# Down-projection weights prepared beside the mixers, and FFN evacuations put ahead, in a one-core hybrid-mixer step

## The chip, the cores and the metric

One core of one Trainium2 chip. The core has a matmul engine (TensorE: PE, with its weight loads PEld), a vector engine (VectorE: DVE), an activation engine (ScalarE: ACT), a general engine (GpSimd: POOL) and SyncE (SP), which in this kernel only issues DMA transfers. The metric is the device time of one execution in microseconds (us); the median of several runs counts.

## The reference

One layer over 2048 prompt tokens behind 16 meta tokens, and over 8 sample sequences of 4 tokens with states of their own. Width 1024. Three mixers run side by side on parts of the projected width, then an output product, then a SwiGLU FFN of inner width 2816:

```python
y, st = _mixer(_rmsnorm(h, norm_mix[l]), p, init_states[l], kv)
h = h + y
h = h + _swiglu(_rmsnorm(h, norm_ffn[l]), w_ffn_in[l], w_ffn_out[l])
...
# _mixer
proj = hn @ w_in
...
oa, s_hgrn_new = _hgrn2_chunked(qa, ka, ai.reshape(B, T, H_A, DV_A), logf, s_hgrn)
...
hm, c_new, n_new, m_new = _mlstm_chunked(qm, km, vm, igate, lfgate, c0, n0, m0)
...
yc = _swa_prompt(qc, kc, vc, sk)          # the sample part: _swa_sample
y = jnp.concatenate([ya, yb, yc], axis=-1) @ w_out
...
# _swiglu
g, u = jnp.split(hn @ w_ffn_in, 2, axis=-1)
return (jax.nn.silu(g) * u) @ w_ffn_out
```

The results are the normalised outputs of prompt and sample tokens, and the mixers' final states.

## The kernel before

The tokens are cut in 17 tiles: tiles 1 to 16 of 128 prompt tokens, and tile 0 with the 32 sample and 16 meta tokens. Large products take fp16 operands, each number split in a high and a low half, in three passes (high·high, high·low, low·high). `split_w` makes the halves: ACT writes the high one, then one DVE operation writes the low one.

The order in time:

1. *Start.* `w_in` is loaded and split.
2. *Mixers.* For each tile, `project(t)` makes the projections, and `mixer_prompt` runs sliding-window attention, mLSTM and HGRN2 as generators, a step of each in turn (`interleave`). The mixed tile `yT` goes to DRAM. Tile 16 comes later.
3. *Out products.* The sample mixer, tile 16's mixer and `out_early` run together. For each pair of tiles `out_product` loads `yT` (as `xT`), multiplies by `w_out` and adds the residual. Seven of the eight pairs are also normalised here, and `prep` makes their FFN operands x2 and stores them. `load_x2` then brings those of group 1 back, by DMA transposes.
4. *FFN*, in three groups of tiles: 1 to 6, 7 to 12, and 13 to 16 with tile 0. Both FFN products are done as Strassen-like 2x2 block products: seven products instead of eight, whose operands are blocks and their sums (`S1` to `S4` of the left operand, `T1` to `T4` of the right one). The inner width has 11 steps `jq` of 256, in parts of 2, 3, 3 and 3. In a part `hidden` (matmuls `s`, evacuated to `tmp`, results hi and lo to `hh`) runs for each of its steps, and then `down` (matmuls `dn`) for both halves `m` of the output and each pair of tiles. So there are four transitions from hidden to down in each group.

In group 1 the weights' operands are made as they are needed. `gu_operands` (gate and up) loads `raw`, forms four sums on POOL (`left`) and splits them: 44 makes, of which two are done before the group. `dn_operands` (down) does the same with `right`: 22 makes. Each has three pairs of ACT and DVE operations of 512, 256 and 1024 columns, and one store of 896 KB to `wgu_scratch` or `wdn_scratch`. Groups 2 and 3 load the operands from there.

The order of the work on each engine is set by a scheduler: it goes by the order in which the program issues the instructions, as far as operands and buffers are there by its own model of time, and what stands inside `tc.high_priority()` goes first. Pools with a fixed number of buffers per tag (`w`: 6, `raw`: 6, `sums`: 2 in group 1) say when a buffer comes free. SP's queue holds nearly all loads and stores in one order.

Lines to follow below: L155 and L156 (`split_w`), L205 (split of an input tile), L1015 to L1018 (`left`) and L1022 to L1025 (`right`) on POOL, L1239 (`s` matmuls), L1244 to L1252 (their evacuation, of which L1248 and L1249 are POOL additions), L1262 (gate times up), L1268 and L1269 (`hh`), L1274 to L1280 (the sums S1 to S4 on POOL), L1292 (`dn` matmuls). In the mixers: L527, L549, L551 and L553 (HGRN2), L835 and L837 (attention's probabilities).

Of the kernel before, what the change touches and what calls it, by code (L numbers as in the profile page):

```python
# [17 lines left out]
P = 128  # L18
# [39 lines left out]

@with_exitstack
def trunk(ctx, tc, I, O, groups):  # L60
    nc = tc.nc
    V, S, G, T = nc.vector, nc.scalar, nc.gpsimd, nc.tensor
    n_names = [0]
# [26 lines left out]
    wdn_d = nc.dram_tensor("wdn_scratch", (NFF // 2, 2, P, 2 * 7 * 256), F16, kind="Internal").ap()  # L90
# [127 lines left out]

    def project(t, s_out):
# [37 lines left out]
        def tl(s, tag, shape, dt=F32, bufs=1):  # L257
            if s.name == "s":
                return at_("s_" + tag, shape, dt)
            return at_(tag, shape, dt, bufs)  # L260
# [117 lines left out]
        with tc.high_priority():  # L378
            for s in segs:
                sl = slice(s.fo, s.fo + s.L)  # L380
                w = NS if s.name == "s" else P
                if s.name == "s":
                    s.vb = at_("s_vb", [NS, 4, 65])
# [6 lines left out]
                V.scalar_tensor_tensor(s.gb, s.gb, 1.0, gB[: s.L], op0=ALU.add, op1=ALU.mult)  # L390
        yield
# [465 lines left out]
    def mixer_prompt(s, yT, off):  # L857
        y = zt("y", [P, 512])
        interleave(swa_prompt(s, yT, off), mlstm_prompt(s, y[:, 256:512]), hgrn_prompt(s, y[:, 0:256]))
        finish_y(y, yT, off, s.L)  # L860

# [228 lines left out]

    smp = sample_mixer(tc, nc, I, O, locals())
# [36 lines left out]
    def kept(dram, make):  # L1128
# [3 lines left out]
        if w_bufs[0] == 6:  # L1132
# [44 lines left out]
    w_gu, w_dn = I["w_ffn_in"][0], I["w_ffn_out"][0]  # L1177

# [30 lines left out]
    with (  # L1209
# [20 lines left out]
        def quad(A, n):  # L1230
# [17 lines left out]
            G.tensor_tensor(r12, r12, r22, op=ALU.add)  # L1248
            G.tensor_tensor(r22, r22, r21, op=ALU.add)  # L1249
            V.tensor_tensor(r11, prod(A12, B21), r11, op=ALU.add)  # L1250
            V.tensor_tensor(r21, prod(A22, T4), r21, op=ALU.add)
            V.tensor_tensor(r12, prod(S4, B22), r12, op=ALU.add)  # L1252
            return r11, r12, r21, r22

        def hidden(q, jq, n):

            sg = quad(gu_first.pop(0) if gu_first else gu_operands(2 * jq * P), n)
            for d in sg:
                S.activation(d, d, AF.Silu, scale=UF)  # L1259
            up = quad(gu_first.pop(0) if gu_first else gu_operands(DFF + 2 * jq * P), n)  # L1260
            for d, v in zip(sg, up):
                V.scalar_tensor_tensor(d, v, UF * HS, d, op0=ALU.mult, op1=ALU.mult)  # L1262
# [3 lines left out]
            def put(op, v):  # L1266
                hi, lo = (hh[a][:, q, op, :n] for a in range(2))
                S.activation(hi, v, AF.Copy)  # L1268
                V.tensor_tensor(lo, v, hi, op=ALU.subtract)  # L1269
# [4 lines left out]
            G.tensor_tensor(s1, a21, a22, op=ALU.add)  # L1274
            put(S1, s1)
            G.tensor_tensor(s2, s1, a11, op=ALU.subtract)
            put(S2, s2)
            G.tensor_tensor(s3, a11, a21, op=ALU.subtract)
            put(S3, s3)
            G.tensor_tensor(s4, a12, s2, op=ALU.subtract)  # L1280
# [426 lines left out]
```

## Time and profile before

| what | value |
|---|---|
| median of 3 runs | 2420.63 us (2420.12 to 2420.94) |
| the profiled execution | 2414.44 us, of which span 2412.7 us |
| mean granted TensorE clock | 0.97 |
| start, projections and mixers of tiles 0 and 1 | the first 100 us |
| mixers of most tiles, 100 to 750 us | 650 us, some 14 tiles |
| last mixers and out products, 750 to 1055 us | 305 us, DMA share 0.68 |
| FFN group 1, 1055 to 1601 us | 546 us |
| FFN group 2, 1601 to 2056 us | 455 us |
| FFN group 3, 2056 us to the end | 357 us |

The profile comes from one execution, 6 us shorter than the median of the runs. The limits of the stages are read from the first matmul of each. Busy time is given per engine and stage; where two stages do the same work, their difference shows what one of them has to wait for. The clock is the share of full speed that TensorE was granted.

### The profile page before, as it was taken

The page shows a single profiled execution, that of the slowest core. Times are in us where ns is not written, and L with a number is a line of the kernel's source. Part 1 is how long each engine was busy: PE and PEld are TensorE (multiplying, and loading weights), DVE is VectorE, ACT ScalarE, POOL GpSimd, SP SyncE. Part 2 cuts the span into 40 slices and gives each one's busy share as a digit, 9 for nine tenths or more (in the row PEclk, how much of TensorE's full clock was granted, in tenths as well). Part 3 has the DMA queues.
Part 4 walks back from the last instruction along what each step waited for, and adds up shares of the span by engine and source line. Part 5 has one row for each costly group of instructions (what it writes and reads, how often), then busy time and mean ns, then how long its engine had stood idle before and what let it go on. Part 6 is the DMA issues. An engine that isn't in the chain of part 4 may idle for free. (4 is left out here: it accounts for less than half of the span.)

```text
span 2412.7 us, 51978 instructions
## 1 busy us (share of the span) xinstructions
PE 2220.3 (92%) x20298; PEld 1607.4 (67%) x20298; DVE 1679.2 (70%) x4030; ACT 943.5 (39%) x2526; POOL 1211.7 (50%) x1629
## 2 busy tenths in 40 slices
PE   6989999999999899896989979889999999999996
PEld 6677767767776445444657556567686767888886
DVE  8788988988988756558879677746454535655546
ACT  7554455554554432334343434422212123332323
POOL 7344344444443464549778788744232324544435
PEclk9999999999999899997999989899999999999998
DMA  7232333333223755996436545684324247744441
GB/s 258 50 63 69 66 67 68 75 61 74 66 64 73 173 183 192 275 330 222 153 139 231 196 158 191 191 287 185 148 108 168 108 152 199 269 176 175 177 174 38
DMA packets 294329, 364.95 MB, mean 151 GB/s; under 512 B 203808, under 2 KB 234480, under 8 KB 294067
## 3 DMA queue, kind: packets, MB, share of 16 engines
q1 hardware_dynamic: 285090, 331.02, 43.6%
q0 software_dynamic: 4384, 15.93, 1.7%
q10 hardware_dynamic: 4608, 14.68, 1.7%
q8 instruction: 159, 2.61, 0.4%
q14 instruction: 88, 0.71, 0.1%
HBM read 212.24 MB, written 103.50 MB: 131 GB/s over the span
## 5 line engine op out<-in xcount | busy, mean ns | idle before, releaser
L1239 PE MATMUL s<-x,w 128*128 128x384 f16 (+1 forms) x5544 | 826.4, 312 | 14.8 <-DMA w<-wgu_scratch 6.2
L1239 PEld LDWEIGHTS <-w 128*128 128x128 f16 x5544 | 542.6, 98 | 296.5 <-issue 13.8
L1292 PE MATMUL dn<-w,hh 128*128 128x256 f16 (+1 forms) x4158 | 444.4, 278 | 56.0 <-ACT hh L1268 23.6
L1292 PEld LDWEIGHTS <-hh 128*128 128x128 f16 (+1 forms) x4158 | 379.6, 99 | 119.8 <-ACT hh L1268 27.8
L212 PEld LDWEIGHTS <-xT 128*128 128x128 f16 (+1 forms) x1992 | 177.4, 99 | 191.4 <-issue 25.2
L1268 ACT ACTIVATE hh<-tmp 128x384 f16<-128x384 f32 (+1 forms) x231 | 112.4, 494 | 280.4 <-DVE tmp L1262 164.5
L1248 POOL TENSOR_TENSOR tmp<-tmp,tmp 128x384 f32<-128x384 f32 (+1 forms) x66 | 65.3, 990 | 279.0 <-ACT tmp L1247 271.8
L1269 DVE TENSOR_TENSOR hh<-tmp,hh 128x384 f16<-128x384 f32 (+1 forms) x231 | 144.5, 633 | 74.2 <-ACT hh L1268 72.5
L212 PE MATMUL wo<-wo,xT 128*128 128x512 f16 x768 | 180.8, 394 | 9.5 <-DVE xn L992 4.6
L156 DVE SCALAR_TENSOR_TENSOR w<-raw,w 128x512 f16<-128x512 f32 (+1 forms) x136 | 111.9, 855 | 7.0 <-ACT w L155 6.9
L1250 DVE TENSOR_TENSOR tmp<-s,tmp 128x384 f32<-128x384 f32 (+1 forms) x66 | 34.2, 518 | 107.3 <-PE s L1239 107.3
L212 PE MATMUL d<-xT,qf 128*128 128x128 f16 (+1 forms) x1632 | 107.7, 220 | 0.0
L156 DVE SCALAR_TENSOR_TENSOR w<-sums,w 128x1024 f16<-128x1024 f32 x68 | 96.9, 1427 | 11.4 <-ACT w L155 11.4
L1259 ACT ACTIVATE tmp<-tmp 128x384 f32<-128x384 f32 (+1 forms) x132 | 61.6, 489 | 107.9 <-DVE tmp L1250 52.6
L212 PE MATMUL d<-xT,bqk 128*128 128x128 f16 (+1 forms) x1632 | 100.6, 221 | 3.2 <-DVE e L278 3.2
L1324 DVE SCALAR_TENSOR_TENSOR xr<-dn,xr 128x256 f32<-128x256 f32 x192 | 78.7, 417 | 34.4 <-PE dn L1292 30.2
L212 PEld LDWEIGHTS <-qf 128*128 128x128 f16 x1632 | 94.4, 100 | 9.1 <-issue 4.1
L212 PEld LDWEIGHTS <-bqk 128*128 128x128 f16 x1632 | 94.0, 100 | 5.4 <-issue 4.5
L212 PE MATMUL d<-xT,cq 128*128 128x128 f16 (+1 forms) x1632 | 96.2, 217 | 0.0
L212 PE MATMUL d<-bvo,xT 128*128 128x512 f16 (+1 forms) x408 | 96.2, 380 | 0.0
L1262 DVE SCALAR_TENSOR_TENSOR tmp<-tmp,tmp 128x384 f32<-128x384 f32 (+1 forms) x132 | 71.9, 558 | 34.1 <-POOL tmp L1249 32.6
L212 PE MATMUL d<-aig,xT 128*128 128x512 f16 (+1 forms) x408 | 92.4, 379 | 3.4 <-DVE g L358 3.4
(536 smaller groups left out, 4064.6 us busy)
## 6 DMA issues: line engine op xcount, KB each, us to landing
w<-wgu_scratch SPq DMA_DIRECT2D x88, 896.0 KB
wgu_scratch<-w SPq DMA_DIRECT2D x44, 896.0 KB
w<-wdn_scratch SPq DMA_DIRECT2D x44, 896.0 KB
raw<-in_w_ffn_in_dram SPq DMA_DIRECT2D x88, 256.0 KB
wdn_scratch<-w SPq DMA_DIRECT2D x22, 896.0 KB
xs<-in_x_prompt_dram SPq DMA_DIRECT2D x26, 512.0 KB
x_scratch<-pT ACTq DMA_DIRECT2D x28, 448.0 KB
raw<-in_w_ffn_out_dram SPq DMA_DIRECT2D x22, 512.0 KB
```

What stands on the lines that cost most here:

```text
L156: V.scalar_tensor_tensor(lo, src, scale, hi, op0=ALU.mult, op1=ALU.subtract)
L212: T.matmul(out, lh(k, a), rh(k, b), start=(n == 0), stop=(n == 3 * nk - 1))
L1239: T.matmul(out, A[k // 2][p][:, a, k % 2 * P : k % 2 * P + P], x2[r][:, k // 2, op, k % 2, :n], start=i == 0, stop=i == 11)
L1248: G.tensor_tensor(r12, r12, r22, op=ALU.add)
L1250: V.tensor_tensor(r11, prod(A12, B21), r11, op=ALU.add)
L1259: S.activation(d, d, AF.Silu, scale=UF)
L1262: V.scalar_tensor_tensor(d, v, UF * HS, d, op0=ALU.mult, op1=ALU.mult)
L1268: S.activation(hi, v, AF.Copy)
L1269: V.tensor_tensor(lo, v, hi, op=ALU.subtract)
L1292: T.matmul(out, hh[p][:, q, a, off : off + L], ws[q][r][:, b], start=(q, p, r) == order[0], stop=(q, p, r) == order[-1])
L1324: V.scalar_tensor_tensor(x[:L, cc], m, UD, x[:L, cc], op0=ALU.mult, op1=ALU.add)
```

## The change

Three things.

*Down weights.* A generator `dn_prep` makes the down operands in 44 pieces of 128 columns. It joins the mixers' generators: `mixer_prompt` of tiles 1 to 15 interleaves three pieces with the three mixers. A piece has three loads (64, 64 and 128 KB) into a tile `nx`, four POOL operations, one ACT and one DVE operation on 128x896, and a store of 448 KB from a tile `nw`; both tiles have one buffer. In group 1 `dn_operands` now loads two halves, like the other groups, and `down` reads them in two runs of 128 columns.

*Room.* To make place, the sample tile's projections are packed in two buffers, stored to DRAM at the end of `project(0)` (`put_away`) and loaded before the sample mixer (`take_back`), into the places of `nx` and `nw`. In the FFN the pool has seven `w` and four `raw` tiles instead of six and six. `load_x2` of group 1 is interleaved with the out products and no longer follows them.

*Priority.* `Ahead` wraps an engine so that each instruction issued through it is inside `tc.high_priority()`; the evacuations, activations and additions of `quad`, `hidden` and `down` go through it, in all three groups. In a profile of the changed kernel these instructions carry the line of the wrapper, L68.

```diff
+class Ahead:
+    def __getattr__(self, name):
+        def op(*a, **k):
+            with self.tc.high_priority():
+                return getattr(self.engine, name)(*a, **k)
+        return op
...
+    VA, SA, GA = (Ahead(tc, e) for e in (V, S, G))
...
+    def put_away():
+        for which, n, c0, c1 in SPK_PARTS:
+            nc.sync.dma_start(smp_d[which, :n, c0:c1], packed[which][:n, c0:c1])
...
+    def dn_prep(n):
+        for jq, m, u in dn_pieces[:n]:
+            x = at_("nx", [P, 8, P])
+            w = at_("nw", [P, 2, 7, P], F16)
+            b12, b11, b21, b22, t1, t2, t3, t4 = (x[:, i] for i in range(8))
...
+            nc.sync.dma_start(b12, rows[0][:, 1])
+            nc.sync.dma_start(b11, rows[0][:, 0])
+            nc.sync.dma_start(x[:, 2:4], rows[1])
+            yield
+            G.tensor_tensor(t1, b12, b11, op=ALU.subtract)
+            G.tensor_tensor(t2, b22, t1, op=ALU.subtract)
+            G.tensor_tensor(t3, b22, b12, op=ALU.subtract)
+            G.tensor_tensor(t4, b21, t2, op=ALU.subtract)
+            yield
+            split_w(x[:, 1:8], w[:, 0], w[:, 1], WS)
+            nc.sync.dma_start(wdn_d[jq, m, u], w.rearrange("p a o c -> p (a o c)"))
+            yield
+        del dn_pieces[:n]
...
-            mixer_prompt(seg_of[t][0], yT, 0)
+            mixer_prompt(seg_of[t][0], yT, 0, *([dn_prep(3)] if t < NTILE - 1 else []))
...
+    take_back(sseg)
     smp = sample_mixer(tc, nc, I, O, locals())
...
-    w_bufs = [6]
+    w_bufs = [7]
...
-        return pg[0].tile([P, 4, 256], F32, tag="raw", bufs=6, name=nm("raw"))
+        return pg[0].tile([P, 4, 256], F32, tag="raw", bufs=4, name=nm("raw"))
...
     def dn_operands(jq, m):
...
-            right(w, sum_tile(), raw[:, 0], raw[:, 1], raw[:, 2], raw[:, 3], raw.rearrange("p (k h) c -> p h k c", k=2)[:, 0], WS)
-        return kept(wdn_d[jq, m], make)
+        w = w_full().rearrange("p a o c -> p (a o c)").rearrange("p (u z) -> p u z", u=2)
+        for u in range(2):
+            nc.sync.dma_start(w[:, u], wdn_d[jq, m, u])
+        return w.rearrange("p u (r o c) -> p u r o c", r=2, o=7)
...
-    interleave(outs)
-    interleave(load_x2(groups[0]))
+    interleave(outs, load_x2(groups[0]))
...
-            S.activation(r11, prod(A11, B11), AF.Copy)
-            V.tensor_tensor(r12, prod(S2, T2), r11, op=ALU.add)
+            SA.activation(r11, prod(A11, B11), AF.Copy)
+            VA.tensor_tensor(r12, prod(S2, T2), r11, op=ALU.add)
...
-            G.tensor_tensor(r12, r12, r22, op=ALU.add)
+            GA.tensor_tensor(r12, r12, r22, op=ALU.add)
...
-            T.matmul(out, hh[p][:, q, a, off : off + L], ws[q][r][:, b], start=(q, p, r) == order[0], stop=(q, p, r) == order[-1])
+            T.matmul(out.rearrange("t (u c) -> t u c", u=2), hh[p][:, q, a, off : off + L], ws[q][:, :, r, b], start=(q, p, r) == order[0], stop=(q, p, r) == order[-1])
```

The order of instructions shows the change at three places. First POOL in group 1, where hidden of steps 5 to 7 ends and down begins (`tmp` are evacuated products, `sums` the weight sums). Before:

```order
L1025 TENSOR_TENSOR sums_20585<-raw_20583,sums_20585 128x256
L1249 TENSOR_TENSOR tmp_20013<-tmp_20013,tmp_20012 128x384
L1022 TENSOR_TENSOR sums_20600<-raw_20598 128x256
L1024 TENSOR_TENSOR sums_20600<-raw_20598 128x256
L1023 TENSOR_TENSOR sums_20600<-raw_20598,sums_20600 128x256
L1022 TENSOR_TENSOR sums_20615<-raw_20613 128x256
L1024 TENSOR_TENSOR sums_20615<-raw_20613 128x256
L1025 TENSOR_TENSOR sums_20600<-raw_20598,sums_20600 128x256
L1023 TENSOR_TENSOR sums_20615<-raw_20613,sums_20615 128x256
L1025 TENSOR_TENSOR sums_20615<-raw_20613,sums_20615 128x256
L1248 TENSOR_TENSOR tmp_20151<-tmp_20151,tmp_20153 128x384
L1249 TENSOR_TENSOR tmp_20153<-tmp_20153,tmp_20152 128x384
```

After (S1 to S3 are the rows that write tmp_20557, tmp_20559 and tmp_20558):

```order
L68 TENSOR_TENSOR tmp_20418<-tmp_20418,tmp_20420 128x384
L68 TENSOR_TENSOR tmp_20420<-tmp_20420,tmp_20419 128x384
L68 TENSOR_TENSOR tmp_20558<-tmp_20558,tmp_20560 128x384
L68 TENSOR_TENSOR tmp_20560<-tmp_20560,tmp_20559 128x384
L68 TENSOR_TENSOR tmp_20557<-tmp_20418,tmp_20420 128x384
L68 TENSOR_TENSOR tmp_20559<-tmp_20417,tmp_20418 128x384
L68 TENSOR_TENSOR tmp_20558<-tmp_20557,tmp_20417 128x384
L1087 TENSOR_TENSOR sums_21367<-raw_21364 128x256
L1089 TENSOR_TENSOR sums_21367<-raw_21364 128x256
L68 TENSOR_TENSOR tmp_20560<-tmp_20419,tmp_20558 128x384
```

The eight sums of the down weights that stood between L1249 of the gate product and L1248 of the up product are gone; two sums of a gate or up make are left, ahead of S4.

Next DVE in the mixer of an early tile (`qz` and `k` are HGRN2's, `dm` and `num` the mLSTM's, `xn` the next input tile; `nw` is a piece's result). Before:

```order
L276 SCALAR_TENSOR_TENSOR q_3029<-tq_3025,xq_3027 128x256
L278 TENSOR_SCALAR e_3031<-d_2928 128x256
L698 TENSOR_TENSOR dm_1928<-sc_1961,dm_1928 128x2x128
L282 RECIPROCAL dd_3034<-dd_3034 128x256
L698 TENSOR_TENSOR dm_1928<-sc_1965,dm_1928 128x2x128
L549 TENSOR_TENSOR qz_465<-qz_465,t_253_1944 64x2x2x32
L205 SCALAR_TENSOR_TENSOR xn_4583<-xs_4574,ss_4579,xn_4583 128x1024
L549 TENSOR_TENSOR qz_465<-qz_465,t_253_1944 64x2x2x32
L551 TENSOR_TENSOR k_730<-k_730,t_253_1944 128x4x32
```

After:

```order
L322 SCALAR_TENSOR_TENSOR q_3095<-tq_3091,xq_3093 128x256
L324 TENSOR_SCALAR e_3097<-d_2994 128x256
L173 SCALAR_TENSOR_TENSOR nw_4470<-nx_4469,nw_4470 128x896
L222 SCALAR_TENSOR_TENSOR xn_4721<-xs_4712,ss_4717,xn_4721 128x1024
L328 RECIPROCAL dd_3100<-dd_3100 128x256
L334 TENSOR_SCALAR f_3105<-dd_3100,omlb_446,lb_444 128x128 x2
L335 TENSOR_SCALAR f_3105<-f_3105 128x256
L747 TENSOR_TENSOR dm_1943<-sc_1979,dm_1943 128x2x128
L747 TENSOR_TENSOR dm_1943<-sc_1983,dm_1943 128x2x128
L598 TENSOR_TENSOR qz_465<-qz_465,t_247_1959 64x2x2x32 x2
L600 TENSOR_TENSOR k_729<-k_729,t_247_1959 128x4x32
L173 SCALAR_TENSOR_TENSOR nw_4598<-nx_4597,nw_4598 128x896
```

Two of the new 128x896 operations stand among the mixers' instructions within twelve rows. Over the whole order, 8 of the 44 pieces stand ahead of the `dm` rows of tile 1, and the other 36 between these and the `dm` rows of tile 10: nine tiles, two to five pieces in each.

Last SP near the end of the out products (`xT` are loads of mixed tiles, the transposes load x2 of group 1, `raw` and `wgu_scratch` belong to the first gate and up weights). Before:

```order
L1057 DMA_TRANSPOSE x_2032_15773<-x_scratch 128x14x128
L1134 DMA wgu_scratch<-w_15826 128x3584
L978 DMA xT_2132_16695<-yT_scratch 128x1024
L978 DMA xT_2133_16696<-yT_scratch 128x1024
L1057 DMA_TRANSPOSE x_2032_15773<-x_scratch 128x14x128
L97 DMA xn_16393<-in_x_sample_dram 32x1024
L98 DMA xn_16393<-in_meta_tokens_dram 16x1024
L1057 DMA_TRANSPOSE x_2033_15774<-x_scratch 128x14x128 x2
L1057 DMA_TRANSPOSE x_2032_15773<-x_scratch 128x14x128
L100 DMA xs_16635<-in_x_prompt_dram 128x1024
L100 DMA xs_16636<-in_x_prompt_dram 128x1024
L1057 DMA_TRANSPOSE x_2032_15773<-x_scratch 128x14x128
```

After:

```order
L1207 DMA wgu_scratch<-w_16353 128x3584
L1129 DMA_TRANSPOSE x_2112_16300<-x_scratch 128x14x128
L1129 DMA_TRANSPOSE x_2113_16301<-x_scratch 128x14x128 x2
L1129 DMA_TRANSPOSE x_2112_16300<-x_scratch 128x14x128 x2
L1129 DMA_TRANSPOSE x_2113_16301<-x_scratch 128x14x128 x2
L1050 DMA xT_2166_16702<-yT_scratch 128x1024
L1050 DMA xT_2167_16703<-yT_scratch 128x1024
L117 DMA xs_16772<-in_x_prompt_dram 128x1024
L1050 DMA xT_2176_16774<-yT_scratch 128x1024
L1050 DMA xT_2177_16775<-yT_scratch 128x1024
L117 DMA xs_16773<-in_x_prompt_dram 128x1024
L1257 DMA raw_17555<-in_w_ffn_in_dram 128x2x256 x2
```

The transposes, which alternated with the last xT loads, now stand together ahead of them, and loads of raw for further weights have moved ahead of the last pairs' xT loads.

More of the change, by code (lines that the diff above doesn't have):

```diff
@@ L56, in bc, with __init__ @@
     return a.to_broadcast(shape)
+class Ahead:
+    def __init__(self, tc, engine):
+        self.tc, self.engine = tc, engine
+    def __getattr__(self, name):
[3 more added lines that the diff above has]
+        return op
 @with_exitstack
@@ L217, in trunk, with in_pack, take_back @@
         pass
+    SPK = {"q": (0, 0, 64), "k": (0, 64, 64), "f": (0, 128, 64), "cin": (0, 192, 224), "cq": (0, 416, 128), "ck": (0, 544, 32),
+           "cv": (0, 576, 128), "g": (0, 704, 8), "va": (0, 712, 256), "ga": (1, 0, 256), "gb": (1, 256, 256), "vb": (1, 512, 260)}
+    SPK_PARTS = ((0, P, 0, 576), (0, NS, 576, 968), (1, NS, 0, 772))
+    SHAPES = {"q": (P, 2, NS), "k": (P, 2, NS), "f": (P, 2, NS), "cin": (P, 4, NB, 7), "cq": (P, 4, NS), "ck": (P, NS),
+              "cv": (NS, P), "g": (NS, 8), "va": (NS, 256), "ga": (NS, 256), "gb": (NS, 256), "vb": (NS, 4, 65)}
+    packed = []
+    def in_pack(tag):
+        which, o, n = SPK[tag]
+        shape = SHAPES[tag]
+        v = packed[which][: shape[0], o : o + n]
+        if len(shape) == 3:
+            return v.rearrange("p (a b) -> p a b", a=shape[1])
+        return v.rearrange("p (a b c) -> p a b c", a=shape[1], b=shape[2]) if len(shape) == 4 else v
+    def put_away():
+        for which, n, c0, c1 in SPK_PARTS:
+            nc.sync.dma_start(smp_d[which, :n, c0:c1], packed[which][:n, c0:c1])
+    def take_back(s):
+        packed[:] = [at_("nx", [P, 1024]), at_("nw", [P, 896])]
+        for which, n, c0, c1 in SPK_PARTS:
+            nc.sync.dma_start(packed[which][:n, c0:c1], smp_d[which, :n, c0:c1])
+        for tag in SPK:
+            setattr(s, tag, in_pack(tag))
     def project(t, s_out):
@@ L258, in tl @@
             if s.name == "s":
-                return at_("s_" + tag, shape, dt)
+                if not packed:
+                    packed.extend(zt(z, [P, 1024]) for z in ("pb0", "pb1"))
+                return in_pack(tag)
             return at_(tag, shape, dt, bufs)
@@ L855, in put_yT, with mixer_prompt @@
         V.scalar_tensor_tensor(lo, pv, scale, hi, op0=ALU.mult, op1=ALU.subtract)
-    def mixer_prompt(s, yT, off):
+    def mixer_prompt(s, yT, off, *others):
         y = zt("y", [P, 512])
-        interleave(swa_prompt(s, yT, off), mlstm_prompt(s, y[:, 256:512]), hgrn_prompt(s, y[:, 0:256]))
+        interleave(swa_prompt(s, yT, off), mlstm_prompt(s, y[:, 256:512]), hgrn_prompt(s, y[:, 0:256]), *others)
         finish_y(y, yT, off, s.L)
+    dn_pieces = [(jq, m, u) for jq in range(NFF // 2) for m in range(2) for u in range(2)]
+    def dn_prep(n):
[3 more added lines that the diff above has]
+            b12, b11, b21, b22, t1, t2, t3, t4 = (x[:, i] for i in range(8))
+            rows = [w_dn[(2 * jq + k) * P : (2 * jq + k + 1) * P, m * 512 : m * 512 + 512].rearrange("p (h u c) -> p h u c", h=2, u=2)[:, :, u] for k in range(2)]
+            nc.sync.dma_start(b12, rows[0][:, 1])
[11 more added lines that the diff above has]
+        del dn_pieces[:n]
     def finish_y(y, yT, off, L):
@@ L1131, in kept @@
         parts = [w[:, 0], w[:, 1]]
[L1132 removed]
+        if w_bufs[0] == 7:
             make(parts)
@@ L1273, in hidden @@
             put(A22, a22)
[L1274 removed]
+            GA.tensor_tensor(s1, a21, a22, op=ALU.add)
             put(S1, s1)
[L1276 removed]
+            GA.tensor_tensor(s2, s1, a11, op=ALU.subtract)
             put(S2, s2)
[L1278 removed]
+            GA.tensor_tensor(s3, a11, a21, op=ALU.subtract)
             put(S3, s3)
[L1280 removed]
+            GA.tensor_tensor(s4, a12, s2, op=ALU.subtract)
             put(S4, s4)
```

64 lines of the change are left out of this document (32 added, 32 removed).

## The prediction

> **What bounds the kernel now.** I read the page's busy line first, then the stretches by stage, then the waits and the clock of the stage that stands out.
>
> ```profile
> PE 2220.3 (92%) x20298; PEld 1607.4 (67%) x20298; DVE 1679.2 (70%) x4030; ACT 943.5 (39%) x2526; POOL 1211.7 (50%) x1629
> ```
>
> PE is the bound on average; the stages differ. Columns of the next view: stretch, length, then busy us and instructions of PE, PEld, DVE, ACT and POOL, granted clock, DMA share, GB/s.
>
> ```profile
> 100.00:750.00 650.00, 604.74 (x7541) 474.44 (x7542) 565.78 (x1819) 332.60 (x1123) 269.60 (x485) 0.99 0.31 67
> ...
> 1055.00:1601.00 546.00, 477.31 (x3244) 322.69 (x3242) 417.94 (x638) 223.11 (x443) 425.47 (x443) 0.94 0.57 196
> 1601.00:2056.00 455.00, 453.62 (x3233) 316.72 (x3234) 220.29 (x428) 107.85 (x235) 154.25 (x179) 0.99 0.47 169
> 2056.00:2412.70 356.70, 337.93 (x3238) 283.38 (x3235) 199.47 (x431) 110.39 (x281) 155.48 (x207) 0.98 0.45 169
> ```
>
> The rows are the mixers, and FFN groups 1, 2, 3. Groups 1 and 2 multiply the same amount (3244 and 3233), and only group 1 makes weights: 546 − 455 = 91 us is what that costs. PE idles 546 − 477.3 = 68.7 there against 1.4, so 67 us of the 91 is waiting; the other 24 is busier PE. By source, first the down and then the hidden products, each in groups 1 and 2:
>
> ```profile
> 1055.00:1601.00 546.00, 174.37 (x1386) 141.39 (x1386) 0.94 0.57 196
> 1601.00:2056.00 455.00, 151.97 (x1385) 135.38 (x1386) 0.99 0.47 169
> ```
> ```profile
> 1055.00:1601.00 546.00, 302.71 (x1848) 180.73 (x1848) 0.94 0.57 196
> 1601.00:2056.00 455.00, 302.79 (x1848) 181.34 (x1848) 0.99 0.47 169
> ```
>
> Hidden costs the same; down costs 22 us more, and the granted clock is why. PE in the stretch about the first transition from hidden to down:
>
> ```profile
> 1117.00:1144.00 27.00, 12.96 (x59) 0.56 0.67 247
> ```
>
> After a long idle stretch PE runs at about half clock. What PE waited for in group 1 (total us, times, longest):
>
> ```profile
> PE dn L1292 <- ACT hh L1268: 23.6, 6, 9.9
> PE dn L1292 <- DVE hh L1269: 11.7, 7, 3.6
> ...
> PE dn L1292 <- DVE w L156: 3.4, 5, 1.5
> PE dn L1292 <- ACT w L155: 2.9, 1, 2.9
> ```
>
> The waits are for the hidden operands hh, not for the weights w. The timeline of the third transition, on POOL, DVE and PE, and then PE at the same place of group 2:
>
> ```profile
> 1380.96 3.51 POOL L1022 TENSOR_TENSOR sums<-raw 128x256 f32<-128x256 f32 x1 [5.08 <-DVE w L156]
> ...
> 1406.23 0.99 POOL L1248 TENSOR_TENSOR tmp<-tmp,tmp 128x384 f32<-128x384 f32 x1
> 1407.30 0.99 POOL L1249 TENSOR_TENSOR tmp<-tmp,tmp 128x384 f32<-128x384 f32 x1
> ```
> ```profile
> 1408.32 0.56 DVE L1262 SCALAR_TENSOR_TENSOR tmp<-tmp,tmp 128x384 f32<-128x384 f32 x1 [4.12 <-POOL tmp L1249]
> ```
> ```profile
> 1404.82 1.04 PE L1292 MATMUL dn<-w,hh 128*128 128x256 f16 x4 [5.75 <-ACT hh L1268]
> 1409.41 8.74 PE L1292 MATMUL dn<-w,hh 128*128 128x256 f16 x55 [3.55 <-DVE hh L1269]
> ```
> ```profile
> 1665.60 21.26 PE L1292 MATMUL dn<-w,hh 128*128 128x256 f16 x191 [0.25 <-DVE hh L1269]
> ```
>
> POOL finishes eight weight sums before the two additions that the up product needs; DVE and PE stand behind them. Group 2, without sums, waits 0.25 us.
>
> **The change, part by part.**
>
> *Group 1.* The 22 down makes leave, and evacuations go first. Group 2 makes no weights, so the rows above price the making: DVE 417.9 − 220.3 = 198 us, POOL 271, ACT 115, for 42 gate and up and 22 down makes. 22 of 64 leave: 68 us of DVE, 93 of POOL, 40 of ACT. The new order has no sum ahead of the additions at the transitions after hidden 5 to 7 and 8 to 10, as in group 2. At the first, sums still stand between the additions that give S1 to S4: I keep 10 us. I keep 5 at the second, where small preparations of group 2 stand, 4 at the last two, 4 in the hidden stretches, 2 for rounding: 25 of the 91 stay, so **−66**. Ends: −91 (all goes) and −30 (only the 35.3 on hh goes, and 5 comes back as waits for evacuations, the next late thing). I take a value nearer −91 because group 2's row shows the same products, with the same additions, without the stalls. The TensorE clock follows idling: the gap of 5.75 us is followed by slow products, so 22 us of the 66 hangs on gaps becoming short.
>
> On SP, 22 raw loads of 512 KB and 22 stores of 896 KB give way to 44 loads of 448 KB: less traffic at a DMA share of 0.57, so 0. Down's moving operand now comes in two runs of 128 columns; no row shows such a product, and with as many columns and instructions as before I take 0.
>
> The Trainium skill ("TensorE: Matmul & The Clock Gate", "HAM oscillation") says that an idle stretch beyond an activity window of about 3.4 us drops the clock to half until a busy one has passed; the 0.56 above agrees. By it, every gap cut below that returns its clock loss whole: the cold share that I keep (22 × 25/91, some 6 us) would go too, and the term would be −72.
>
> *Mixers.* 44 pieces come in: each adds 4 POOL operations of 128x128, one ACT and one DVE of 128x896, three loads and a store. Nearest rows of the mixers:
>
> ```profile
> L835 ACT ACTIVATE ph<-pb 128x1024 f16<-128x1024 f32 x28 | 29.6, 1056 | 28.4 <-DMA pT<-ph 8.6 <-POOL ga L373 8.2 <-POOL pb L834 6.1
> ...
> L205 DVE SCALAR_TENSOR_TENSOR xn<-xs,ss,xn 128x1024 f16<-128x1024 f32 x12 | 15.3, 1278 | 2.9 <-ACT xn L203 2.9
> ...
> L205 DVE SCALAR_TENSOR_TENSOR yh<-y,yh 128x512 f16<-128x512 f32 x14 | 9.6, 688 | 0.4 <-ACT yh L203 0.4
> ...
> L553 POOL TENSOR_TENSOR t<-f 128x128 f32<-128x128 f32 x14 | 6.5, 465 | 8.1 <-DVE Sst L599 8.0
> ```
>
> Between 688 ns at 512 and 1278 at 1024, 896 columns come to 1.13 us; 44 × 1.13 = 50 us of DVE. ACT: 44 × 0.94 = 41 us, under 332.6 busy of 650, hidden. POOL: 176 × 0.465 = 82 us, covered as work under 269.6 of 650, but DVE and POOL slow each other:
>
> ```profile
> 400.11 0.29 DVE L551 TENSOR_TENSOR k<-k,t 128x128 f32<-128x128 f32 x1
> ...
> 407.29 2.27 DVE L551 TENSOR_TENSOR k<-k,t 128x128 f32<-128x128 f32 x1
> ```
> ```profile
> 407.27 2.13 POOL L837 TENSOR_TENSOR ph<-pb,ph 128x1024 f16<-128x1024 f32 x1 [0.92 <-ACT ph L835]
> ```
>
> The same operation takes 0.29 us at 400.11, and 2.27 with a long POOL operation. I take a fifth of the 82 us as such collisions (nothing to half is possible): 16. So DVE gains 66 us, and 36 of the 44 pieces stand in nine tiles: 54 us, 6.0 a tile. A tile's period is 650/14 = 46.4 us, with (650 − 565.8)/14 = 6.0 us of idle DVE and 3.2 of idle PE. DVE is on the way to PE here:
>
> ```profile
> PE lv L527 <- DVE k L551: 21.5, 19, 3.8
> ```
>
> Filling all of DVE's idle time would need an order without dependences, so I let a third be absorbed: **+36**. Ends: +10 (DVE's idle takes nearly all) and +74 (36/44 of 50 and of half the 82, nothing absorbed). A piece's store waits for its DVE operation on SP; behind it stand the next x tile, loaded a tile early, and the next piece's loads: 46 us of period cover these.
>
> *Start and out products.*
>
> ```profile
> 0.00:50.00 50.00, 35.24 (x677) 34.31 (x678) 42.65 (x108) 38.20 (x83) 37.35 (x53) 0.93 0.85 306
> 50.00:100.00 50.00, 45.43 (x501) 31.23 (x500) 34.76 (x147) 26.68 (x94) 24.77 (x52) 1.00 0.23 49
> ```
> ```profile
> 975.00:1055.00 80.00, 64.43 (x468) 32.32 (x467) 37.24 (x44) 21.58 (x35) 35.25 (x46) 0.87 1.00 285
> ```
>
> A piece moves 0.7 MB (256 KB in, 448 out): 2.3 us at 306 GB/s, in a start that DMA fills to 0.85. Eight pieces stand in the first 100 us; with one buffer they come one after the other, most of them in the second 50, where DVE has 15 us and DMA most of its time free: **+3** (0 to +18 for eight). At the end of the out products DMA is full (1.00). The x2 transposes now stand on SP ahead of five tiles' xT loads instead of among them, and up to three more operand tiles of 1.4 MB (5 us each at 285 GB/s) come before the last xT: **+5** (−10, since group 1 may start earlier, to +25). The packed sample tensors are 0.5 MB out and back, under 2 us each at that rate, far from their use: 0, covered by the mixers' DMA share of 0.31.
>
> *Groups 2 and 3.* Two half loads replace one, under a PE that is busy 453.6 of 455: 0 (−2 to +5, if SP's issue became late).
>
> Sum: −66 + 36 + 3 + 5 = −22, from the profiled execution's 2414.44 (span 2412.7) to 2392.4. The median of the runs, 2420.63, is 6.2 above that execution, and I add this to each time: 2399.
>
> **The rivals.**
>
> *B, the mixers swallow it.* For it: POOL and ACT are half idle, and 3.2 us of PE slack a tile. Against it: DVE at 0.87 is the engine that PE waits for. With +10 in place of +36: 2373.
>
> *C, DVE and POOL shut each other out.* POOL's operations each stop DVE for their length: half of 82 us, 41, joins the 50, and with 36/44 of that and no absorption the mixers cost +74: 2437, slower. For it: the pair at 407.3, and POOL's 3.51 us at 1380.96, where its neighbours take about 1. Against it: POOL already works 269.6 us in the mixers, and DVE still reaches 0.87. It decides once the mixers cost over 58 us (66 less 8), 6.4 a tile: a period above 52.8 us in the nine tiles. The Trainium skill ("SBUF — State Buffer", "SBUF: two separate sides") states this rule: DVE and GpSimd share a port pair as an exclusive lock, the first holds it through its instruction, and the other blocks wholly. The pair at 407.3 agrees.
>
> *D, group 1 keeps its stalls.* The change does not do what it says: 44 gate and up makes remain, raw shrinks from six to four, so that only two makes are loaded ahead, and a started POOL sum cannot be overtaken. Against it: the new order at the later transitions. With −30 in place of −66: 2435.
>
> **How the numbers follow.** The measurement tells about 0.2%, 5 us, from no change. The forecast has 0.50 (own range 2383 to 2417: mixers ±12, group 1 ±10), B 0.20, C 0.18, D 0.12. Faster: 0.45 of the forecast and all of B, 0.65. Same: the forecast's upper tail 0.05, and 0.03 each of C and D, 0.11. Slower: 0.24. The range 2362 to 2440 holds the forecast, most of B, and the lower halves of C and D; about 0.17 is left out.
>
> **What would show it.** Group 1 should take about 480 us from the first hidden product to group 2, with PE idle below 20 us, down products within 8 us of group 2's and waits on hh below 10. The nine tiles with pieces should have a period of about 50.5 us and the others 46; the new DVE rows of 128x896 near 1.1 us. The stretch before group 1 should grow by no more than 10 us. The forecast is wrong if the period passes 52.8 us (C), if it stays below 48 (B), or if group 1 still idles 40 us (D).

## The result: 3% slower, and the profile after

The changed kernel takes 2492.73 us (median of four runs) against 2420.38 for the kernel before in the same session: the ratio is 1.0296, 95% interval 1.0278 to 1.0314. The forecast was 2399. The profiled executions differ by nearly as much (spans 2490.6 and 2412.7), so their stages can be compared. The marks are the first `dm` products on DVE of two tiles and the first hidden matmul of each FFN group. The first two marks are called tile 1 and tile 15, as in the expectations below. By the shapes of their rows both names, and the tile 10 named ahead of the prediction, are one too high: the first is the `dm` of the 16 meta tokens (16x32), the second that of tile 14. The tiles between them are the same before and after:

| stretch | before | after | difference | forecast |
|---|---|---|---|---|
| start to tile 1's `dm` | 94.4 | 122.7 | +28.3 | +3 |
| tile 1 to tile 15 | 635.3 | 713.7 | +78.4 | +36 |
| tile 15 to group 1 | 325.6 | 358.4 | +32.8 | +5 |
| group 1 | 546.8 | 484.7 | −62.1 | −66 |
| groups 2 and 3 | 810.7 | 811.1 | +0.4 | 0 |

Group 1 came as forecast. First the groups 1 and 2 of the changed kernel by stretches (columns as in the prediction), then the down products alone in both, then what PE waited for in group 1:

```profile
1194.80:1679.50 484.70, 459.02 (x3244) 317.92 (x3243) 339.43 (x564) 180.01 (x369) 315.13 (x341) 0.98 0.55 188
1679.50:2133.70 454.20, 453.90 (x3234) 316.82 (x3235) 220.21 (x428) 107.34 (x233) 153.49 (x177) 1.00 0.48 167
```
```profile
1194.80:1679.50 484.70, 158.40 (x1386) 136.60 (x1386) 0.98 0.55 188
1679.50:2133.70 454.20, 152.12 (x1386) 135.44 (x1386) 1.00 0.48 167
```
```profile
PE dn L1358 <- DMA w<-wdn_scratch: 8.5, 2, 7.1
PE s L1305 <- DMA w<-wgu_scratch: 6.0, 1, 6.0
PE dn L1358 <- ACT hh L68: 2.9, 1, 2.9
...
PE dn L1358 <- DVE hh L68: 2.2, 3, 1.1
```

PE idles 25.7 us instead of 68.7, the waits on hh are 5.1 instead of 35.3, and the down products cost 6 us more than in group 2 instead of 22: with the gaps the half clock went too. All that was lost was lost ahead of group 1. From tile 1's `dm` to group 1 both kernels issue nearly the same matmuls, before and after:

```profile
94.40:1055.30 960.90, 875.68 (x9485) 622.93 (x9483) 767.46 (x2294) 441.47 (x1409) 419.15 (x709) 0.97 0.42 108
```
```profile
122.70:1194.80 1072.10, 912.07 (x9454) 655.51 (x9453) 810.34 (x2341) 475.21 (x1450) 515.80 (x867) 0.91 0.47 126
```

The stretch is 111 us longer. PE idles 160.0 us in it instead of 85.2, and is busy for 36 us more with nearly the same work: the granted clock fell from 0.97 to 0.91. The border at tile 15 isn't sharp: up to it the changed kernel has issued 7722 matmuls, the kernel before 7372. The difference is most of one more tile's projections, which PE now does ahead of this mark: 472 us of projections against 441. A sharper border is the `dm` of tile 16 (at 837.1 and 953.2 us), by which both kernels have done all projections. The rows up to it and from it to group 1, before and after:

```profile
94.40:837.10 742.70, 683.82 (x8235) 522.93 (x8234) 643.16 (x2067) 374.98 (x1254) 312.01 (x558) 0.99 0.34 75
837.10:1055.30 218.20, 191.86 (x1254) 100.00 (x1253) 124.30 (x227) 66.49 (x156) 107.14 (x151) 0.93 0.72 218
```
```profile
122.70:953.20 830.50, 735.00 (x8293) 559.03 (x8293) 675.03 (x2107) 401.96 (x1285) 389.22 (x701) 0.93 0.41 100
953.20:1194.80 241.60, 177.07 (x1165) 96.48 (x1164) 135.31 (x235) 73.25 (x165) 126.58 (x166) 0.83 0.68 212
```

So 88 of the 111 us are lost in the mixers and 23 behind them. Of the 88, 37 are idle PE (58.9 to 95.5 us) and 51 are busier PE, at a clock of 0.93 instead of 0.99. The experiments below are judged by the whole, from tile 1 to group 1.

Three places show where the time went. At the start, PE, then POOL, then ACT:

```profile
56.11 6.79 PE L229 MATMUL d<-xT,bqk 128*128 128x128 f16 x96 [29.60 <-ACT cin L351]
```
```profile
52.16 1.15 POOL L206 TENSOR_TENSOR bvo<-pb,bvo 128x512 f16<-128x512 f32 x1
53.25 0.28 POOL L347 MEMSET pb<- 128x224 f32 x1
```
```profile
53.57 0.29 ACT L348 ACTIVATE pb<-d 128x128 f32<-128x128 f32 x1 [1.26 <-POOL pb L347]
```

The packed sample projections lie in `pb0` and `pb1`, in which the weight load also stages `w_in`. The packing begins only when the last staged piece (`bvo`, at 52.16) has been read; until then the projections' results stay in PSUM, and PE stands for 29.6 us.

At the end of the out products, one row of PE's waits from 836 us to group 1:

```profile
PE wo L229 <- DMA xT<-yT_scratch: 42.4, 1, 42.4
```

From 1062.8 to 1122.9 us SP issues twelve x2 transposes, with raw loads and four weight stores among them; the next xT load stands behind all of these and is issued at 1125.3. The transposes occupy SP for 1.7 to 6.6 us each, 36 in all, and the weight stores stand 19.5 us until DVE has written their low halves. What the transposes wait for, the profile doesn't name.

In the mixers, a piece at 282 us, on POOL, ACT and DVE:

```profile
281.95 0.46 POOL L924 TENSOR_TENSOR nx<-nx 128x128 f32<-128x128 f32 x1 [1.32 <-DMA nx<-in_w_ffn_out_dram]
284.20 0.45 POOL L925 TENSOR_TENSOR nx<-nx 128x128 f32<-128x128 f32 x1 [1.79 <-DMA nx<-in_w_ffn_out_dram]
```
```profile
285.51 0.95 ACT L172 ACTIVATE nw<-nx 128x896 f16<-128x896 f32 x1 [2.06 <-POOL nx L927]
```
```profile
286.49 1.09 DVE L173 SCALAR_TENSOR_TENSOR nw<-nx,nw 128x896 f16<-128x896 f32 x1 [3.02 <-ACT nw L172]
```

The third load was issued 2.4 us after the first, behind a transpose. POOL, ACT and DVE each stood at their own instruction of the piece until it could run, with the mixers' next instructions behind it in the same queue. For the nine tiles with pieces (122.7 to 597.5 us), grouped:

```profile
L173 DVE SCALAR_TENSOR_TENSOR nw<-nx,nw 128x896 f16<-128x896 f32 x36 | 39.7, 1102 | 22.6 <-ACT nw L172 22.6
...
L172 ACT ACTIVATE nw<-nx 128x896 f16<-128x896 f32 x36 | 34.1, 946 | 44.4 <-POOL nx L927 44.3
```

These nine tiles take 52.8 us each, against 44.9 before; the five behind them take 47.8 against 46.2. The period stands on the bound of 52.8 that the prediction set for rival C. But the projections that came forward are in the 52.8, and the bound was worked out from a period of 46.4.

### The profile page after: what moved, and what is told of

The parts are those of the page before. It is cut to its first block, busy times and chain, and to the rows that moved or that the text cites. A ratio compares the mean times of both kernels' runs of the same rounds, so it can differ in the third digit from the quotient of the medians.

```text
span 2490.6 us, 52419 instructions
## 1 busy us (share of the span) xinstructions
PE 2238.9 (90%) x20298; PEld 1635.0 (66%) x20298; DVE 1655.3 (66%) x4008; ACT 941.9 (38%) x2504; POOL 1209.8 (49%) x1718
## 5 line engine op out<-in xcount | busy, mean ns | idle before, releaser
L68 POOL TENSOR_TENSOR tmp<-tmp,tmp 128x384 f32<-128x384 f32 (+3 forms) x424 | 390.9, 929 | 587.1 <-ACT tmp L68 350.0
L1358 PE MATMUL dn<-w,hh 128*128 128x256 f16 (+1 forms) x4158 | 428.4, 274 | 20.6 <-DMA w<-wdn_scratch 8.5
L68 DVE TENSOR_TENSOR tmp<-s,tmp 128x384 f32<-128x384 f32 (+1 forms) x330 | 169.6, 517 | 321.3 <-PE s L1305 290.9
L68 ACT ACTIVATE hh<-tmp 128x384 f16<-128x384 f32 (+1 forms) x231 | 112.2, 494 | 237.3 <-DVE tmp L68 138.1
L68 DVE TENSOR_TENSOR hh<-tmp,hh 128x384 f16<-128x384 f32 (+1 forms) x231 | 146.6, 642 | 62.9 <-ACT hh L68 60.6
L68 ACT ACTIVATE tmp<-dn 128x256 f32<-128x256 f32 (+1 forms) x184 | 68.7, 378 | 219.6 <-PE dn L1358 202.0
L68 ACT ACTIVATE tmp<-s 128x384 f32<-128x384 f32 (+1 forms) x132 | 59.5, 456 | 228.0 <-PE s L1305 227.8
L68 DVE TENSOR_TENSOR xr<-xr,tmp 128x256 f32<-128x256 f32 (+1 forms) x216 | 120.7, 569 | 6.4 <-POOL tmp L68 0.6
L229 PE MATMUL d<-xT,bqk 128*128 128x128 f16 (+1 forms) x1632 | 96.7, 219 | 29.6 <-ACT cin L351 29.6
L68 ACT ACTIVATE tmp<-tmp 128x384 f32<-128x384 f32 (+1 forms) x132 | 62.0, 490 | 120.3 <-DVE tmp L68 98.9
L68 DVE SCALAR_TENSOR_TENSOR xr<-dn,xr 128x256 f32<-128x256 f32 x192 | 79.0, 417 | 37.4 <-PE dn L1358 32.7
L602 POOL TENSOR_TENSOR t<-t 128x8 f32<-128x8 f32 (+2 forms) x100 | 26.4, 264 | 153.8 <-DVE k L600 114.9
```

The lines of the kernel that those rows point to most:

```text
L68: return getattr(self.engine, name)(*a, **k)
L229: T.matmul(out, lh(k, a), rh(k, b), start=(n == 0), stop=(n == 3 * nk - 1))
L602: G.tensor_tensor(tn, tv[:, :, :, 0], tv[:, :, :, 1], op=ALU.mult)
L1358: T.matmul(out.rearrange("t (u c) -> t u c", u=2), hh[p][:, q, a, off : off + L], ws[q][:, :, r, b], start=(q, p, r) == order[0], stop=(q, ...
```

## The experiments

"Tile 1 to group 1" is 961 us in the kernel before. All rows are of profiled executions, except the medians.

| run | median | tile 1's `dm` at | tile 1 to tile 15 | tile 1 to group 1 | group 1 |
|---|---|---|---|---|---|
| before | 2420 | 94.4 | 635 | 961 | 547 |
| after | 2493 | 122.7 | 714 | 1072 | 485 |
| start_own | 2486 | 102.4 | 720 | 1087 | 491 |
| x2_last | 2477 | 124.9 | 710 | 1048 | 487 |
| prio_only | 2421 | 96.5 | 637 | 962 | 550 |
| no_ahead | 2489 | 122.9 | 706 | 1066 | 485 |
| both | 2468 | 102.3 | 723 | 1066 | 489 |
| one_load | 2442 | 102.1 | 706 | 1044 | 484 |
| no_sums | 2458 | 104.5 | 713 | 1055 | 485 |
| no_lo | 2400 | 95.7 | 663 | 988 | 502 |
| pinned | 2443 | 94.3 | 717 | 1045 | 488 |
| pool_lo | 2443 | 95.4 | 712 | 1041 | 493 |
| pool_lo_pinned | 2436 | 95.2 | 703 | 1033 | 490 |
| spread | 2504 | 95.3 | 641 | 963 | 635 |
| half | 2410 | 95.1 | 667 | 998 | 509 |

**Start (start_own).**

```diff
-                    packed.extend(zt(z, [P, 1024]) for z in ("pb0", "pb1"))
+                    packed.extend([at_("nx", [P, 1024]), at_("nw", [P, 896])])
```

> The changed kernel, but the packed sample projections lie from the start in the places of the pieces' two tiles and not in two staging buffers of the weight load. Theory A (PE's 29.6 us wait at the start is for buffers that the weight load still uses): tile 1's dm rows come near 97 instead of 122.7 us, the wait for cin is below 5 us, and the run is some 25 us shorter than the changed kernel's 2492, 2465 to 2470. Theory B (the pieces themselves, or their DMA, delay the start): dm of tile 1 stays above 115 us and the time within 8 us of 2492.

Tile 1's `dm` came at 102.4 instead of 122.7 and the wait for `cin` was gone: theory A of the wait holds. The time did not follow (2486; its two runs, 2479 and 2493, are too far apart to tell a gain). Pieces now begin later: of the eight that stood in the start two are left, and six stand in the mixers. The stretch to group 1 grew by 14.5 us, the wait for xT to 50.7 us, and group 1 by 6.

**x2 loads (x2_last).**

```diff
-    interleave(outs, load_x2(groups[0]))
+    interleave(outs)
+    interleave(load_x2(groups[0]))
```

> The changed kernel, but the loads of x2 for group 1 follow the out products again and are not interleaved with them. Theory A (the 42.4 us wait of PE for xT comes from the x2 transposes that stand ahead of xT in SP's queue, each waiting for a store of ACT's queue): the stretch from the last mixer's rows to group 1 shortens by 25 to 35 us, the wait for xT falls below 8 us, the time is 2457 to 2467. Theory B (the stretch is longer because DMA moves more, or because the sample mixer's reloads come late): less than 10 us of change.

The stretch shortened by 24.6 us and the run by 16; PE's waits before group 1 are now

```profile
PE wo L229 <- DVE xs L1070: 24.9, 4, 12.6
...
PE wo L229 <- DMA xT<-yT_scratch: 10.1, 1, 10.1
```

The order on SP made the wait, as theory A has it; time and wait (10.1, not below 8) fell short of it, since a part of the wait became one for the residual tiles. That the transposes waited for stores of ACT's queue isn't shown.

**Priority alone (prio_only) and the move alone (no_ahead).**

```diff
 prio_only: the kernel before, and
+    VA, SA, GA = (Ahead(tc, e) for e in (V, S, G))
 ... used in quad, hidden and down as in the change
```

> The kernel before, with only the priority of evacuations and activations; the down weights are still made in group 1. Theory A (POOL, DVE and ACT have room in group 1 for all makes, 426 of 546 us at most, and only the order caused the stalls): group 1 takes 485 to 500 us, the run 2360 to 2375. Theory B (the makes must leave, since the sums of the down weights are then late for down itself): group 1 takes 525 to 560 us and PE waits for w, the run 2400 to 2435.

```diff
 no_ahead: the changed kernel, and
-    VA, SA, GA = (Ahead(tc, e) for e in (V, S, G))
+    VA, SA, GA = V, S, G
```

> The changed kernel without the priority; the down weights stay beside the mixers. Theory A (order causes the stalls; with the down sums gone the scheduler has little left to put ahead): group 1 takes 490 to 505 us, the run 2495 to 2512. Theory B (moving the makes alone gives the whole gain): 485 us, and 2490 to 2495. If the priority is what counts, group 1 takes above 520 us and the run above 2525.

Priority alone gave a ratio of 1.0011 (0.9994 to 1.0027). Its waits in group 1 are those of before:

```profile
PE dn L1307 <- ACT hh L68: 24.2, 7, 10.0
PE dn L1307 <- DVE hh L68: 11.7, 7, 3.6
```

By its time priority alone follows theory B, but not for B's reason: PE waits 6.3 us for w, as before. Without priority group 1 took 485.1 us, as with it (theory B of that run). So the gain of group 1 owes nothing to priority; it came with the makes that left. The pools of seven `w` and four `raw` tiles changed with them and were not run alone. I did not expect that priority would do nothing. A likely reason, not tested: a sum whose data are there is placed while the hidden's addition still waits for its product, and priority doesn't make the addition ready.

**The base for the mixers (both).** Both edits above together.

> The changed kernel with both edits of the first runs: sample projections packed in the pieces' tiles from the start, and x2 loaded after the out products. If their effects add, the start stays near 102 us to tile 1's dm rows, the wait for xT below 12 us, and the time is 2468 to 2476; if the pieces that the start no longer holds cost the same in the mixers, 2470 to 2480 with the stretch from tile 1 to tile 15 (dm rows to dm rows) at 720 us against 635 before. This is the base of the next three.

2468 and 1066 us: the two add. What is left of the loss is 8 us at the start and 105 us from tile 1 to group 1.

**What a piece costs (one_load, no_sums, no_lo).** Each takes one part out of all 44 pieces of the base.

```diff
 one_load: a single nx tile, loaded for the first piece only
+            if (jq, m, u) == (0, 0, 0):
                 nc.sync.dma_start(b12, rows[0][:, 1])
 ...
 no_sums: a single nx tile, zeroed once
-            G.tensor_tensor(t1, b12, b11, op=ALU.subtract)
 ... and the three others
 no_lo: a single nw tile, zeroed once
-            split_w(x[:, 1:8], w[:, 0], w[:, 1], WS)
+            S.activation(w[:, 0], x[:, 1:8], AF.Copy, scale=WS)
```

> As the base, but only the first piece is loaded, and all others work on the same data (their results are not the weights): sums, split and store of each piece stay. Theory A (a piece costs its DVE operation, 1.1 us, plus the time for which queues stand behind a piece whose loads have not landed): the stretch from tile 1 to tile 15 falls from some 720 to 680 to 695 us. Theory B (POOL's sums and DVE shut each other out): it stays at 710 or above.

> As the base, but without the four POOL sums of each piece (the operand's sum part is left at zero). Theory A (work of DVE and waits for loads): the stretch from tile 1 to tile 15 falls by 15 us at most, to 705 to 718. Theory B (the sums shut DVE out for half their length, 41 us): it falls by 30 to 45 us, to 675 to 690.

> As the base, but without the DVE operation of each piece (the low halves are left at zero). Theory A (DVE is on the way to PE: its 1.1 us and its wait for ACT, 0.6 us, are paid by each piece): the stretch from tile 1 to tile 15 falls by 55 to 75 us, to 645 to 665. Theory C (DVE's operation fits its idle time, and POOL's and ACT's waits carry the cost): it falls by less than 25 us.

From tile 1 to group 1 the loads are worth 22 us (1066 to 1044), the sums 11 (to 1055), the DVE operation 78 (to 988): 111 in sum, against the 105 to be explained. By the expectations' own stretch the numbers are 17, 10 and 60. The sums decide against rival C here: without them the stretch keeps nine tenths of its excess. The loads lie between the two theories, short of A's 28 to 43. The DVE operation is theory A's. The base and the run without low halves:

```profile
102.30:1168.30 1066.00, 915.62 (x9453) 658.90 (x9454) 806.06 (x2346) 482.05 (x1456) 542.61 (x889) 0.92 0.49 130
```
```profile
95.70:1083.70 988.00, 885.02 (x9475) 629.65 (x9471) 789.10 (x2297) 473.59 (x1450) 498.26 (x877) 0.97 0.52 135
```

44 operations of 1.1 us are 48 us, and they cost 78. Of these, 13 come back in group 1 (502 us without the operations, 489 with them), where the run without low halves makes three gate and up operands that the base makes ahead of the group. Up to the `dm` of tile 16 the cost is 65 (840.8 us with them, 776.0 without): 20 of idle PE and 45 of busier PE, as the clock is 0.93 there with them and 0.97 without (67 more matmuls are in it). In the base DVE also stood for the piece's ACT operation:

```profile
DVE nw L173 <- ACT nw L172: 18.3, 10, 5.3
```

How much of this wait is price isn't shown: without the sums it is 39.3 us, and the stretch is still shorter.

**Place (pinned).** The first sum, the ACT and the DVE operation of each piece are held behind what was issued before them on their engine; three pieces stand in each of 15 tiles.

```diff
+            tc.keep_in_program_order(G.tensor_tensor(t1, b12, b11, op=ALU.subtract))
 ...
+            tc.keep_in_program_order(S.activation(w[:, 0], x[:, 1:8], AF.Copy, scale=WS))
+            tc.keep_in_program_order(V.scalar_tensor_tensor(w[:, 1], x[:, 1:8], WS, w[:, 0], op0=ALU.mult, op1=ALU.subtract))
```

> As the base with both edits, but each piece's first sum, its ACT and its DVE operation are held behind what the program issued before them on their engine, two steps after its loads: three pieces in each of 15 tiles instead of all early, and loads have time to land. Theory A (a piece costs its DVE work, 1.1 us, and the rest, 0.8 us, is queues that stand behind late loads or ACT): the stretch from tile 1 to tile 15 falls from 723 to 685 to 705 us, DVE's wait for a piece's ACT operation from 18 us to below 6. Theory B (the place does not matter, the work of four engines does): 715 or above.

The stretch to tile 15 was 717: theory B, 2 us above its bound, as most of the price stays wherever the pieces stand. DVE's wait for ACT fell from 18.3 to 11.5 us only. The start was back at 94.3 us, and tile 1 to group 1 took 1045, 21 less than the base. This run isolates the price: 0 at the start, +84 to group 1, −59 in group 1, and 24 us slower in the profile (2436.9 against 2412.7). All of the 84 is lost by the `dm` of tile 16. Behind it, as in the changed kernel and the base, stand three gate and up makes that the kernel before does in group 1, so a part of the 59 may be theirs.

**DVE's part given to POOL (pool_lo, pool_lo_pinned).**

```diff
+            S.activation(x[:, 0:4], x[:, 0:4], AF.Copy, scale=WS)
 ...
-            split_w(x[:, 1:8], w[:, 0], w[:, 1], WS)
+            S.copy(w[:, 0], x[:, 1:8])
+            G.tensor_tensor(w[:, 1], x[:, 1:8], w[:, 0], op=ALU.subtract)
```

> As the base, but DVE has no part in the pieces: ACT scales the loaded blocks in place (one more ACT operation of 128x512), and POOL subtracts for the low half (128x896), with the same result. Theory A (DVE's work is what cannot be absorbed): the stretch from tile 1 to tile 15 is 660 to 680 us, near the 663 of the run without low halves, and the time 2396 to 2412, below the kernel before. Theory B (POOL's work shuts DVE out, or POOL becomes late for its own mixer steps): 700 us or more, and above 2430.

> The same without DVE, with the pieces held at three a tile as in the pinned run. Theory A: the waits behind late loads go too, the stretch is 650 to 670 us and the time 2388 to 2405. If the place matters only through DVE, it equals the unpinned one within 6 us; if POOL's longer operations come in the way of mixer steps wherever they stand, it is no better than 2415.

Theory B held: 1041 us, where the run without low halves takes 988. DVE's row shows why:

```profile
95.40:1135.90 1040.50, 915.27 (x9483) 653.51 (x9482) 843.52 (x2297) 498.38 (x1494) 579.47 (x922) 0.94 0.48 129
```

DVE issues the same 2297 instructions as without low halves and is busy 843.5 us instead of 789.1; up to tile 15 it is 629.6 instead of 574.3. The new POOL operation, up to tile 15:

```profile
L931 POOL TENSOR_TENSOR nw<-nx,nw 128x896 f16<-128x896 f32 x41 | 78.7, 1920 | 17.2 <-ACT nw L930 16.6 <-ACT dg L560 0.6
```

So 79 us of POOL lengthened DVE's instructions by 55. Rival C's mechanism is strong for these operations; in the change, with its short sums, it is a small part. The Trainium skill ("SBUF — State Buffer", "SBUF: two separate sides") has an exclusive lock there; the trace agrees in kind, and seven tenths of POOL's time is what it cost. Held in place, the same pieces cost 8 us less; at 2436 us they are no better than the 2415 of their expectation, so these operations are in the way wherever they stand.

**Is the price fixed, and must the makes leave (half, spread)?**

```diff
 half: pinned, two pieces a tile, of the first output half only
+    dn_pieces = [(jq, 0, u) for jq in range(NFF // 2) for u in range(2)]
 ... dn_operands(jq, 1) makes and stores its operand in group 1 as before
 spread: the kernel before, in group 1
                     hidden(jq - q0, jq, n)
+                    if gi == 0 and jq + 1 < q1:
+                        ws0.append(dn_operands(jq, 0))
+                        if jq + 2 == q1:
+                            ws0.append(dn_operands(jq + 1, 0))
 ... first sum of each down make: tc.keep_in_program_order(first); w 7, raw 4
```

> As the pinned run, but only the 22 pieces of the first output half stand beside the mixers, two a tile; the 11 makes of the second half are done in group 1 as before. From tile 1's dm rows to group 1 the kernel before takes 961 us and the pinned run 1045. Theory A (each piece is paid in full, since DVE, PE and POOL wait for one another in every tile): 998 to 1010. Theory B (idle time takes up the first pieces, and only the dense ones are paid, as the prediction's third absorbed supposes): 966 to 988. Group 1 should take 500 to 520 us, since half of the sums are gone from the transitions; so the run is 2405 to 2425 under A and 2375 to 2400 under B.

> The kernel before, nothing beside the mixers and no priority; in group 1 the down operands of the first output half are asked for after each hidden step (the last one's before it), the first sum of each down make is held behind what POOL was given before, and the pool has seven w and four raw tiles as in the changed kernel. Theory A (the stalls are down sums that stand on POOL ahead of hidden's additions, and their order alone is enough): waits on hh fall from 35 us to below 15, group 1 takes 505 to 525 us, the run 2378 to 2400. Theory B (POOL and DVE have too much to do in group 1 wherever it stands, 426 and 418 us of 546): what hh gains, w loses; group 1 takes 535 to 560 us and the run 2410 to 2435.

`half` took 998 us to group 1: 36.6 us for 22 pieces, 1.66 each, against 83.7 for 44, 1.90 each, in the pinned run. Theory A holds at its edge, with two pieces a tile instead of three. Up to the `dm` of tile 16 the pinned run and `half` read:

```profile
94.30:922.40 828.10, 723.60 (x8325) 545.80 (x8324) 689.93 (x2112) 411.37 (x1297) 411.93 (x734) 0.95 0.43 108
```
```profile
95.10:870.30 775.20, 698.61 (x8205) 537.88 (x8203) 676.29 (x2085) 391.54 (x1275) 355.43 (x644) 0.96 0.39 91
```

Against the 742.7 us of the kernel before that is 85.4 and 32.5 us, 1.9 and 1.5 a piece. In the pinned run 45.6 us of it are idle PE and 39.8 busier PE, in `half` 17.7 and 14.8. Group 1 took 509: 38 of the 62 us are gained with half of the makes still in it, those that are needed later in each part. The run is 2409.5 us, and its ratio to the kernel before 0.995 (0.9934 to 0.9967): by the medians it is half a per cent faster than the kernel before. The two profiled executions are alike (spans 2411.5 and 2412.7).

`spread` failed on group 1's hidden products:

```profile
PE s L1241 <- ACT w L155: 100.0, 7, 17.7
PE dn L1294 <- ACT w L155: 21.0, 4, 7.0
PE dn L1294 <- ACT hh L1270: 4.6, 3, 3.0
```

The waits on hh went, from 35 us to below 10, as theory A has it, but the down makes now took the place of the gate and up makes that hidden needs: 100 us. Group 1, 635 us, and the run, 2504, lie above the ranges of both theories. It changed order, place in the program and pool sizes together, so it shows that this order is bad, not that none would do.

## Why the prediction was wrong

*Group 1, −66, measured −62.* Right, in size and mechanism: group 2's row was the right yardstick, 16 of the 22 us of slow clock went with the gaps, and the remainder (25 forecast, 30 measured) moved to waits for loaded operands. A part may be work done earlier: 25 of the 64 makes left the group, not 22, since three gate and up makes now stand ahead of it. The rank of causes was wrong: the prediction spoke of makes that leave and evacuations that go first; the second did nothing.

*Mixers, +36, measured +78 to tile 15 and +88 to the end of the mixers, and the step that failed.* The sum had DVE's operation (1.13 us forecast, 1.10 measured) and its number right, and the collisions with POOL near enough (16 forecast; without low halves DVE is busy 22 us more for nearly the same instructions). Its terms are 1.5 us a piece, and 1.0 with a third absorbed. Three steps were wrong.

The first is "I let a third be absorbed": in the price nothing was. A piece cost 1.5 to 1.7 us with two a tile, 1.9 with three, and 2.4 in the base. The reading that fits: DVE's idle 6.0 us a tile were not free room. In the kernel before, from 100 to 750 us, 36 of the 61 us of DVE's waits whose end the profile names end with PE, these first:

```profile
DVE kb L781 <- PE cu L779: 12.5, 7, 2.6
DVE qz L549 <- PE lv L527: 7.1, 8, 1.9
```

PE in turn waits for DVE in the row that the prediction quoted (L527 for L551). Work put into a chain of two engines that wait for each other lengthens the chain; no run tests this reading by itself.

The second is missing from the sum altogether: the wait of POOL, ACT and DVE in turn for a piece whose loads had not landed, which the prediction covered with "46 us of period". The period covers the next x tile, not the instructions queued behind the piece. Loads are worth 22 us, and DVE's wait for ACT was 18 to 23.

The third is the clock, for which the sum has no term, and it is the largest. PE's idle time in the mixers grew by 37 us, close to the 36 of the forecast, but this is luck, since the waits behind late loads are in it. The other 51 us are busier PE.

*The clock.* It was read for group 1 and forgotten in the mixers. In the mixers it fell from 0.99 to 0.93. The share not granted is 7 us of 743 before and 58 of 830 after, which is the size of the 51 us that PE is busier (58 more matmuls are in it). What let the clock fall, and how far a slower PE lengthens the waits in turn, no run separates: clock and waits come and go together.

*Start, +3, measured +28.* The term counted the pieces' DMA. The packing into `pb0` and `pb1` was costed by its 0.5 MB and called far from its use; that these are the weight load's staging buffers was in the code, and the buffer's release at 52 us was not looked up.

*Out products, +5, measured +33.* The mechanism was named (transposes and raw loads ahead of xT on SP) and priced by bytes, 5 us a tile of operands. The price is the wait of the queue: SP issues nothing for xT from 1063 to 1125 us, while transposes occupy it and weight stores stand for DVE. Behind the `dm` of tile 16 the loss is 23, and x2_last takes back 21 of it there (25 from tile 1 to group 1); the rest of the 33 belongs to the mixers.

*Rivals.* C had the time nearest to the result, 2437, still 56 us short. That its 74 in the mixers comes close to 78 is luck, since its mechanism is too small: without the sums only 11 of 105 us went. B, with 10 us in the mixers, is refuted; so is D, with 30 gained in group 1.

## What to carry to other kernels

Idle time of an engine inside a chain of engines that wait for each other is not room for more work: read who ends the idle time before you fill it. An instruction that waits in an in-order queue, as here on POOL, ACT, DVE and SP, holds everything behind it, so side work needs its loads well ahead, and a price counted in bytes or busy time is too low wherever a queue or a buffer's release is the wait. Give side work its own buffers, and move only the part whose removal ends a stall: here half of the pieces won 38 of the 62 us for 37 of the 84. And read the clock in each stage that gets new waits, not only in the one that is to gain.

## What was not expected of the hardware

The POOL operations of 128x896 with two SBUF inputs (1.92 us each) took 55 us from DVE in 79, while the four 128x128 sums of a piece (0.5 us each) took some 18 in 85: here long POOL operations cost DVE more than short ones of the same total. And the granted clock was 0.94 over tiles 1 to 15 of the base, where PE was busy 649 of 723 us (0.99 before, with 589 of 635): it fell in a stage in which PE looks nearly full. The longest wait doesn't tell: in the changed kernel PE's longest wait there is 3.0 us at a clock of 0.95, and in the kernel before one of 3.8 us went with 0.99.
